# A hybrid encoder block on one core: the linear attention's decays move from the states to the queries, and the key norms' input moves to another ring

## The chip, the core and the metric

The kernel runs on one core of one Trainium2 chip. The metric is the device time of the whole program in microseconds (us). TensorE (PE) multiplies matrices into PSUM; VectorE (DVE), ScalarE (ACT) and GpSimd (POOL) work element by element; SyncE (SP) issues the DMAs here, all in one queue, in order. In the profile PEld is the loading of PE's weights.

## The reference

One layer of an encoder: 1024 tokens of width 1024, float32. Two branches work on the same normed projection, a linear attention with decays (4 heads, both directions) and a windowed attention (8 query heads, 2 key heads); their gated sum goes through a projection, and a SwiGLU network follows. What matters here is the linear attention and the norm of the windowed keys:

```python
    b = jnp.cumsum(log_g, axis=3)
    ...
    q_dec = q * jnp.exp(b)
    k_inv = k * jnp.exp(-b)
    k_tail = k * jnp.exp(b_last - b)
    ...
    def step(state, inp):
        kv_n, dec_n = inp
        return dec_n[..., None] * state + kv_n, state
    _, states = lax.scan(step, jnp.zeros(...), (chunk_kv, chunk_decay))
    o_inter = jnp.einsum("bhncd,nbhde->bhnce", q_dec, states)
    ...
    k = _rope(_rms_norm(k.astype(f32).reshape(bsz, s, hkv, hd), k_g), pos)
```

A query meets the state of the chunks before it (behind it, in the backward direction). The state is a 128x256 matrix for each head; each of its 128 rows has its own decay.

## The kernel before

Products run in pairs of `fp32r` parts: a weight unit (`wr`, 128x512) is split into `wh` by ScalarE and `wl` by VectorE, and three matmuls make one product. PE's instructions stand in the order in which the code is written; on the other engines a scheduler sets the order.

The stage of the change is the linear attention, about 338 to 557 us of the span. It goes by heads (`hd`, 4) and by chunks of 128 tokens (`c`, 8 a head), 32 in all, in numbered slots. In slot `n` stand `g_gates` for an even chunk and its neighbour (a pair shares `qk`, `e`, `cs`, `sm`, `q2`), one slot on `g_powers`, two on `g_scores`, four on `g_out`. When the last chunk of a head is through, `g_back_out` goes back over its chunks, and `g_turn` transposes the results `ob` two by two and writes them out by way of `ot`. Each slot is filled with matmuls of the projections that the next stages need (`fill`, 24 to 8 a slot, the list `dense`); these are the rows `mm<-wh,xh` and their like. So PE has work in every slot, but in a fixed order: where a matmul of the attention waits for its operand, all that is behind it waits too.

What the change touches:
- `sm` holds, for each pair, direction and chunk, the log decay from the edge of the chunk to its middle and from the middle to the other edge. Queries and keys are scaled with respect to the middle (`q2`, `en`).
- Forward, `g_out` makes `dec`, the decay from the middle of the chunk before to the middle of this one (one exponential of a column on ScalarE, L719), scales the state `pf` with it into `th` (ScalarE, L721), multiplies `th` by `q2[0]` (PE), and carries the state on: `pf = pf * dec + kv` (VectorE, L722).
- Backward, `g_back` does the same with `decb` (L741), `thb` (L743) and `kb` (L745), and `g_back_out` multiplies `thb` by `q2[1]`.
- `k_norm(t)` (eight of them, planned for slots 36 to 43) loads the keys of 128 tokens from `skv` into `kvr`, a ring of two buffers of its own (L784), norms and turns them on ScalarE and VectorE (L787 to L801), and writes `key` (L803). Since `kvr` is a ring of its own, the scheduler starts them as soon as `skv` is there; in the profile they run from 363 to 464 us.
- `qk` is the ring of two buffers into which `g_gates` loads a pair's queries and keys; `g_powers` reads it last.

Of the kernel before, what the change touches and what calls it, by code (L numbers as in the profile page):

```python
# [11 lines left out]
AF = mybir.ActivationFunctionType  # L12
ALU = mybir.AluOpType

P = 128
# [15 lines left out]
def body(tc, i, out):  # L31
    nc = tc.nc
    with ExitStack() as root:
# [8 lines left out]
        def nm(s):  # L42
            uid[0] += 1
            return f"{s}_{uid[0]}"
# [4 lines left out]
        def chtile(shape, dt=F32):  # L49
            return psc.tile(list(shape), dt, tag="ch", name=nm("ch"))  # L50
# [24 lines left out]
        def mm(o, a, b, start, stop):  # L75
            nc.tensor.matmul(o, a, b, start=start, stop=stop)  # L76

        def mm3(o, ah, al, bh, bl, start, stop):
            mm(o, ah, bh, start, False)
            mm(o, ah, bl, False, False)  # L80
            mm(o, al, bh, False, stop)
# [13 lines left out]
        def rsqrt(dst, v, scale, epsv, eps_t, pool, shape, tag, tags=None):  # L95
            tags = tags or (tag + "l", tag + "t")
            l = pool.tile(list(shape), F32, tag=tags[0], name=nm("rl"))
            nc.scalar.activation(l, v, AF.Ln, bias=eps_t[:, 0:1], scale=scale)
            nc.scalar.activation(l, l, AF.Exp, scale=-0.5)
            t = pool.tile(list(shape), F32, tag=tags[1], name=nm("rt"))  # L100
            nc.vector.tensor_scalar(t, v, scale, epsv, op0=ALU.mult, op1=ALU.add)
            nc.vector.tensor_tensor(t, t, l, op=ALU.mult)
            nc.vector.scalar_tensor_tensor(t, t, -0.5, l, op0=ALU.mult, op1=ALU.mult)
            nc.vector.scalar_tensor_tensor(dst, t, 1.5, l, op0=ALU.add, op1=ALU.mult)
# [10 lines left out]
        scr = {}  # L115
# [425 lines left out]
        with tc.manual_schedule(engines={mybir.EngineType.PE}):  # L541
# [8 lines left out]
            for k in range(KT):  # L550
# [5 lines left out]
                c = slice((k % 4) * P, (k % 4 + 1) * P)  # L556
# [63 lines left out]
        def gtile(tag, shape=(P, 256), dt=F32, bufs=2):  # L620
            return gt.tile(list(shape), dt, tag=tag, name=nm(tag), bufs=bufs)

        gla = {}
# [38 lines left out]
        def g_powers(hd, c):  # L662

            pr = gla[hd, c].pr
            qk, e, cs = pr.qk, pr.e, pr.cs
            ef, csf = (v.rearrange("p d j t -> p (d j t)") for v in (e, cs))
            nc.vector.tensor_tensor(e[:, 0], cs[:, 0], cs[:, 0, :, 63:64].to_broadcast([P, 2, P]), op=ALU.subtract)
            nc.vector.tensor_tensor(e[:, 1, :, 1:P], cs[:, 1, :, 0:P - 1], cs[:, 1, :, 63:64].to_broadcast([P, 2, P - 1]),
                                    op=ALU.subtract)
            nc.vector.tensor_scalar(e[:, 1, :, 0:1], cs[:, 1, :, 63:64], -1.0, None, op0=ALU.mult)  # L670

            x1 = cs.rearrange("p d j t -> p d (j t)")
            x2 = e.rearrange("p d j t -> p d (j t)")
            nc.scalar.activation(csf, ef, AF.Exp, scale=-1.0 / 16)
            nc.scalar.activation(ef, ef, AF.Exp, scale=1.0 / 16)
            pr.en = gtile("en", (P, 2, 256))
            nc.vector.tensor_tensor(pr.en[:, 0], x2[:, 0], qk[:, 1], op=ALU.mult)
            nc.vector.tensor_tensor(pr.en[:, 1], x1[:, 1], qk[:, 1], op=ALU.mult)
            pr.q2 = (gtile("q2f", bufs=3), gtile(f"q2b{c}", bufs=(3, 2, 2, 1)[c // 2]))
            nc.vector.tensor_tensor(pr.q2[0], x1[:, 0], qk[:, 0], op=ALU.mult)  # L680
            nc.vector.tensor_tensor(pr.q2[1], x2[:, 1], qk[:, 0], op=ALU.mult)
# [26 lines left out]
        def g_out(hd, c):  # L708

            a = gla[hd, c]  # L710
            kv = chtile((P, 2, 256))
            for d in range(2):
                mm3(kv[:, d], a.kth[:, d], a.ktl[:, d], a.vh, a.vl, True, True)
            a.pf = gtile("pf")
            if c:
                pf = gla[hd, c - 1].pf
                dec = gtile("dec", (P, 1))
                p = gla[hd, c - 1]
                nc.scalar.activation(dec, a.pr.sm[:, 0, a.j, 0:1], AF.Exp, bias=p.pr.sm[:, 0, p.j, 1:2])  # L719
                th = gtile("th")  # L720
                nc.scalar.activation(th, pf, AF.Copy, scale=dec[:, 0:1])  # L721
                nc.vector.scalar_tensor_tensor(a.pf, pf, dec[:, 0:1], kv[:, 0], op0=ALU.mult, op1=ALU.add)  # L722
                a.kb = gtile(f"kb{c}", bufs=2 if c < 5 else 1)
                nc.scalar.copy(a.kb, kv[:, 1])
            else:
                nc.vector.tensor_copy(a.pf, kv[:, 0])
                a.kb = None
            o = chtile((P, 256))
            mm3(o, a.sh, a.sl, a.vh, a.vl, True, c == 0)
            if c:  # L730
                mm(o, a.pr.q2[0][:, a.t], th, False, True)
            a.ob = gtile(f"ob{c}", bufs=2 if c < 5 else 1)
            nc.scalar.copy(a.ob, o)

        def g_back(hd, c):

            a = gla[hd, c]
            if c < NC - 1:
                n = gla[hd, c + 1]
                dec = gtile("decb", (P, 1))  # L740
                nc.scalar.activation(dec, a.pr.sm[:, 1, a.j, 1:2], AF.Exp, bias=n.pr.sm[:, 1, n.j, 0:1])  # L741
                a.thb = gtile("thb")
                nc.scalar.activation(a.thb, n.kb, AF.Copy, scale=dec[:, 0:1])  # L743
                if c:
                    nc.vector.scalar_tensor_tensor(a.kb, n.kb, dec[:, 0:1], a.kb, op0=ALU.mult, op1=ALU.add)  # L745

        def g_back_out(hd, c):
            a = gla[hd, c]
            if c < NC - 1:
                o2 = chtile((P, 256))  # L750
                mm(o2, a.pr.q2[1][:, a.t], a.thb, True, True)
                nc.vector.tensor_tensor(a.ob, a.ob, o2, op=ALU.add)
            if c:
                g_back(hd, c - 1)

            if c % 2:
                a.ss = gtile("oss", (P, 2))
            ss = a.ss if c % 2 else gla[hd, c + 1].ss
            sq = gtile("osq", bufs=1)
            nc.scalar.activation(sq, a.ob, AF.Square, accum_out=ss[:, 1 - c % 2:2 - c % 2])  # L760
            if c % 2 == 0:
                rs = gtile("ors", (P, 2))
                rsqrt(rs, ss, 1.0 / 256, EPS, epst, gt, (P, 2), "on")
                for j, v in enumerate((gla[hd, c + 1].ob, a.ob)):
                    nc.scalar.activation(v, v, AF.Copy, scale=rs[:, j:j + 1])
# [14 lines left out]
        def k_norm(t):  # L780

            need(("skv", t))
            raw = gtile("kvr", (P, 2, P))
            nc.sync.dma_start(out=raw.rearrange("p a b -> p (a b)"), in_=scr["skv", t][:, 0:256])  # L784
            b = gtile("sq2", (P, 2, P), bufs=1)
            ss = gtile("ss2", (P, 2))
            nc.scalar.activation(b, raw, AF.Square)  # L787
            nc.vector.tensor_reduce(ss, b, axis=mybir.AxisListType.X, op=ALU.add)
            rs = gtile("rs2", (P, 2))
            rsqrt(rs, ss, 1.0 / 128, EPS, epst, gt, (P, 2), "sn2")  # L790
            qn = gtile("qn2", (P, 2, P))
            for h in range(2):
                nc.vector.scalar_tensor_tensor(qn[:, h], raw[:, h], rs[:, h:h + 1], tb[0], op0=ALU.mult, op1=ALU.mult)
            c = tb[1][:, t:t + 1].to_broadcast([P, 2, 64])
            s = tb[2][:, t:t + 1].to_broadcast([P, 2, 64])
            nc.vector.tensor_tensor(b[:, :, 0:64], qn[:, :, 64:128], s, op=ALU.mult)
            nc.vector.tensor_tensor(b[:, :, 64:128], qn[:, :, 0:64], s, op=ALU.mult)
            nc.vector.tensor_tensor(qn[:, :, 0:64], qn[:, :, 0:64], c, op=ALU.mult)
            nc.vector.tensor_tensor(qn[:, :, 64:128], qn[:, :, 64:128], c, op=ALU.mult)
            nc.vector.tensor_tensor(qn[:, :, 0:64], qn[:, :, 0:64], b[:, :, 0:64], op=ALU.subtract)  # L800
            nc.vector.tensor_tensor(qn[:, :, 64:128], qn[:, :, 64:128], b[:, :, 64:128], op=ALU.add)  # L801
            scr["key", t] = scratch(f"key_{t}", (P, 256))
            nc.sync.dma_start(out=scr["key", t], in_=qn.rearrange("p a b -> p (a b)"))  # L803
# [3 lines left out]
        for n in range(NH * NC):  # L807
            hd, c = divmod(n, NC)
# [11 lines left out]
        with tc.manual_schedule(engines={mybir.EngineType.PE}):  # L820
            fill(24)
            for t in range(last + 1):
                n = 24 if t < 2 else 16 if t < 4 else 12 if t < NH * NC + 4 else 8 if t < last - 1 else 18
# [189 lines left out]
        for n in range(2 * KT):  # L1013
            g, t = divmod(n, KT)
# [522 lines left out]
```

## Time and profile before

| what | value |
|---|---|
| time, median of 3 runs | 1645.47 us (1645.38 to 1646.94) |
| the profiled execution's own time | 1645.61 us |
| its span, first to last instruction | 1643.8 us |
| granted TensorE clock | 1.000 |
| `th` (L721) and `thb` (L743), ScalarE, 28 each | 515 and 510 ns (medians) |
| `pf` (L722), 28, and `kb` (L745), 24, VectorE | 476 and 482 ns (medians) |
| bytes moved | 262.91 MB, mean 160 GB/s |

How to read it: a row of the timeline has start and duration in us, engine, line, operation, written tile `<-` read tiles, and in brackets how long the engine sat idle before it and who ended that. In a group's row stand the count, busy us and mean ns. A line such as L76 or L72 is that of a helper (`mm`, `wunit`), so that the tiles' names tell what is meant.

### The profile page before, as it was taken

How to read it: one execution, taken by the hardware profiler on the slowest of the kernel's cores; microseconds unless marked ns; L12 is line 12 of the kernel's file. 1: busy time of each engine (PE TensorE's matmuls, PEld its weight loads, DVE VectorE, ACT ScalarE, POOL GpSimd, SP SyncE). 2: the span in 40 equal slices, each digit the busy share in tenths (PEclk: the TensorE clock that was granted, in tenths of full speed). 3: DMA queues.
4: the chain of work that ended last, by engine and by line, in shares of the span. 5: the costliest groups of instructions: out<-in, count | busy, mean ns of one | idle time of the engine just before them, and what ended most of it. 6: DMA issues, size and time to landing. Idle time of an engine off the chain costs nothing.

```text
span 1643.8 us, 23281 instructions
## 1 busy us (share of the span) xinstructions
PE 1626.0 (99%) x7588; PEld 1346.0 (82%) x7588; DVE 1251.4 (76%) x2559; ACT 842.6 (51%) x1762; POOL 76.0 (5%) x68
## 2 busy tenths in 40 slices
PE   9999999999999989999999999999999999999999
PEld 7888888888888778888888888888888888888887
DVE  8866665589986598867885678887777778779655
ACT  8622224468998666665554557333333333354442
POOL 0000000000000034540000000000000000000000
PEclk9999999999999999999999999999999999999999
DMA  7554334475554633248765544443334443596433
GB/s 238 176 178 148 115 122 135 173 250 173 179 161 129 191 108 97 77 138 280 225 205 175 168 146 145 140 149 109 109 115 147 142 147 129 177 341 193 149 98 119
DMA packets 168010, 262.91 MB, mean 160 GB/s; under 512 B 19324, under 2 KB 52860, under 8 KB 167888
## 3 DMA queue, kind: packets, MB, share of 16 engines
q1 hardware_dynamic: 167888, 261.42, 49.8%
q8 instruction: 60, 0.98, 0.2%
q14 instruction: 62, 0.51, 0.1%
HBM read 187.93 MB, written 73.42 MB: 159 GB/s over the span
## 4 chain that ended last, share of the span: by engine, by line
PE 84%; DVE 9%; ACT 4%; DMA 2%; issue 1%; POOL 1%; SPq 0%; ACTq 0%; DVEq 0%
PE mm L76 23%; PE mm L306 9%; PE mm L308 9%; PE mm L307 9%; PE mm L1350 7%; PE ch L1350 5%; PE ch L76 4%; PE ch L306 4%; PE ch L308 4%; PE ch L307 4%; PE ch L460 3%; PE mm L460 2%; ACT p L956 1%; DVE wl L72 1%; DVE cs L655 1%
## 5 line engine op out<-in xcount | busy, mean ns | idle before, releaser
L298 ACT ACTIVATE wh<-ws 128x512 fp32r<-128x512 f32 x132 | 83.3, 632 | 195.9 <-PE mm L307 102.2
L70 ACT ACTIVATE wh<-wr 128x512 fp32r<-128x512 f32 x202 | 124.9, 626 | 87.4 <-PE mm L76 54.9
L72 DVE TENSOR_TENSOR wl<-wr,wh 128x512 fp32r<-128x512 f32 x202 | 137.7, 686 | 26.8 <-ACT wh L70 26.4
L299 DVE TENSOR_TENSOR wl<-ws,wh 128x512 fp32r<-128x512 f32 x132 | 90.5, 686 | 22.7 <-ACT wh L298 22.6
L298 ACT ACTIVATE wh<-wr 128x512 fp32r<-128x512 f32 x69 | 43.6, 632 | 124.8 <-issue 49.7
L962 POOL TENSOR_SCALAR p<-p,rd 128x384 f32<-128x384 f32 (+1 forms) x64 | 75.8, 1202 | 657.1 <-DMA qr<-sq 587.2
L298 ACT ACTIVATE wh<-a 128x512 fp32r<-128x512 f32 x64 | 40.5, 633 | 91.4 <-PE ch L1350 42.3
L76 PE MATMUL mm<-wh,xl 128*128 128x512 f32 x192 | 83.1, 433 | 0.0
L76 PE MATMUL mm<-wh,xh 128*128 128x512 f32 x192 | 79.6, 415 | 0.0
L76 PE MATMUL mm<-wl,xh 128*128 128x512 f32 x192 | 79.6, 414 | 0.0
L299 DVE TENSOR_TENSOR wl<-a,wh 128x512 fp32r<-128x512 f32 x64 | 44.2, 691 | 43.1 <-ACT wh L298 42.5
L1350 PE MATMUL mm<-hh,wh 128*128 128x512 f32 x176 | 68.5, 389 | 0.0
L1350 PE MATMUL mm<-hl,wh 128*128 128x512 f32 x176 | 68.5, 389 | 0.0
L1350 PE MATMUL mm<-hh,wl 128*128 128x512 f32 x176 | 68.5, 389 | 0.0
L76 PE MATMUL mm<-xl,wh 128*128 128x512 f32 x160 | 64.5, 403 | 0.1
L76 PE MATMUL mm<-xh,wh 128*128 128x512 f32 x160 | 64.4, 403 | 0.2 <-ACT wh L70 0.2
L76 PE MATMUL mm<-xh,wl 128*128 128x512 f32 x160 | 59.2, 409 | 0.0
L1320 DVE TENSOR_TENSOR hl<-hr,hh 128x512 fp32r<-128x512 f32 x75 | 51.4, 685 | 3.7 <-ACT hh L1319 3.7
L1350 PE MATMUL ch<-hh,wh 128*128 128x512 f32 x132 | 51.3, 389 | 0.0
L1350 PE MATMUL ch<-hl,wh 128*128 128x512 f32 x132 | 51.3, 389 | 0.0
L1350 PE MATMUL ch<-hh,wl 128*128 128x512 f32 x132 | 51.3, 389 | 0.0
L76 PE MATMUL mm<-oah,wh 128*128 128x512 f32 x128 | 50.2, 392 | 0.0
(620 smaller groups left out, 5077.7 us busy)
## 6 DMA issues: line engine op xcount, KB each, us to landing
wr<-in_w_fi_dram SPq DMA_DIRECT2D x102, 256.0 KB
wr<-in_w_f_dram SPq DMA_DIRECT2D x80, 256.0 KB
wr<-in_w_t_dram SPq DMA_DIRECT2D x56, 256.0 KB
B<-c SPq DMA_DIRECT2D x44, 256.0 KB
T<-tx SPq DMA_DIRECT2D x44, 256.0 KB
a<-in_w_fo_dram SPq DMA_DIRECT2D x44, 256.0 KB
hr<-T SPq DMA_DIRECT2D x44, 256.0 KB
wr<-in_w_ob_dram SPq DMA_DIRECT2D x32, 256.0 KB
```

Source lines behind the costliest of these rows:

```text
L70: nc.scalar.activation(h, raw, AF.Copy)
L72: nc.vector.tensor_tensor(l, raw, h.bitcast(F32), op=ALU.subtract)
L76: nc.tensor.matmul(o, a, b, start=start, stop=stop)
L298: nc.scalar.activation(h, src, AF.Copy)
L299: nc.vector.tensor_tensor(l, src, h.bitcast(F32), op=ALU.subtract)
L306: nc.tensor.matmul(o, h[:, c], x[kk][0], start=start and kk == 0, stop=False, skip_group_check=True)
L307: nc.tensor.matmul(o, h[:, c], x[kk][1], start=False, stop=False, skip_group_check=True)
L308: nc.tensor.matmul(o, l[:, c], x[kk][0], start=False, stop=kk == nk - 1, skip_group_check=True)
L460: nc.tensor.matmul(ys[m], a[:, c], b, start=f0, stop=f1, skip_group_check=True)
L962: nc.gpsimd.tensor_scalar(p[:, h, :w], p[:, h, :w], rd[:, h:h + 1], None, op0=ALU.mult)
L1320: nc.vector.tensor_tensor(l, r, h.bitcast(F32), op=ALU.subtract)
L1350: nc.tensor.matmul(ys[m], a[:, c], b, start=f0, stop=f1, skip_group_check=True)
```

## The change

The decays of a pair, forward and backward, are now made in `g_powers`, in one tile `dec`: two small sums on VectorE (one in the first pair of a head) and one exponential on ScalarE. `g_out` and `g_back` no longer scale the state. They multiply the 128x128 block of queries in place by the same column (VectorE), behind the scores that read it unscaled, and PE multiplies it by the unscaled state `pf` or `kb`. `k_norm` loads all 512 columns of `skv` into a buffer of the ring `qk` and uses the first 256; `kvr`, `th`, `thb` and `decb` are gone.

```diff
@@ g_powers
+            pr.dec = gtile("dec", (P, 2, 2), bufs=16)
+            nc.vector.tensor_tensor(pr.dec[:, 1], pr.sm[:, :, 1, 0], pr.sm[:, :, 0, 1], op=ALU.add)
+            if c:
+                nc.vector.tensor_tensor(pr.dec[:, 0], pr.sm[:, :, 0, 0], gla[hd, c - 1].pr.sm[:, :, 1, 1], op=ALU.add)
+            dc = pr.dec[:, 0 if c else 1:2]
+            nc.scalar.activation(dc, dc, AF.Exp)
@@ g_out
-                dec = gtile("dec", (P, 1))
-                p = gla[hd, c - 1]
-                nc.scalar.activation(dec, a.pr.sm[:, 0, a.j, 0:1], AF.Exp, bias=p.pr.sm[:, 0, p.j, 1:2])
-                th = gtile("th")
-                nc.scalar.activation(th, pf, AF.Copy, scale=dec[:, 0:1])
-                nc.vector.scalar_tensor_tensor(a.pf, pf, dec[:, 0:1], kv[:, 0], op0=ALU.mult, op1=ALU.add)
+                dec = a.pr.dec[:, a.j, 0:1]
+                q = a.pr.q2[0][:, a.t]
+                nc.vector.tensor_scalar(q, q, dec, None, op0=ALU.mult)
+                nc.vector.scalar_tensor_tensor(a.pf, pf, dec, kv[:, 0], op0=ALU.mult, op1=ALU.add)
...
-                mm(o, a.pr.q2[0][:, a.t], th, False, True)
+                mm(o, q, pf, False, True)
@@ g_back
-                dec = gtile("decb", (P, 1))
-                nc.scalar.activation(dec, a.pr.sm[:, 1, a.j, 1:2], AF.Exp, bias=n.pr.sm[:, 1, n.j, 0:1])
-                a.thb = gtile("thb")
-                nc.scalar.activation(a.thb, n.kb, AF.Copy, scale=dec[:, 0:1])
+                dec = (n if a.j else a).pr.dec[:, 1 - a.j, 1:2]
+                q = a.pr.q2[1][:, a.t]
+                nc.vector.tensor_scalar(q, q, dec, None, op0=ALU.mult)
+                a.after = n.kb
                 if c:
-                    nc.vector.scalar_tensor_tensor(a.kb, n.kb, dec[:, 0:1], a.kb, op0=ALU.mult, op1=ALU.add)
+                    nc.vector.scalar_tensor_tensor(a.kb, n.kb, dec, a.kb, op0=ALU.mult, op1=ALU.add)
@@ g_back_out
-                mm(o2, a.pr.q2[1][:, a.t], a.thb, True, True)
+                mm(o2, a.pr.q2[1][:, a.t], a.after, True, True)
@@ k_norm
-            raw = gtile("kvr", (P, 2, P))
-            nc.sync.dma_start(out=raw.rearrange("p a b -> p (a b)"), in_=scr["skv", t][:, 0:256])
+            qk = gtile("qk", (P, 2, 256))
+            raw = qk[:, 0].rearrange("p (a b) -> p a b", a=2)
+            nc.sync.dma_start(out=qk.rearrange("p a b -> p (a b)"), in_=scr["skv", t])
```

PE's order stays, but for the names of two operands a chunk and a handful of neighbouring rows; on ACT there are 1534 rows where there were 1630. What follows shows the scheduler's order, without times.

First ScalarE in the middle of the stage (second head's forward pass, first head's return; in the trace of before 402.7 to 406.5 us). Before:

```order
L733 COPY ob_930_4156<-ch_4151 128x256
L99 ACTIVATE rl_4117<-rl_4117 128x2
L741 ACTIVATE decb_4401<-sm_3274 128x1
L724 COPY kb_928_4149<-ch_4136 128x256
L695 ACTIVATE kth_4168<-ch_4165 128x256
L721 ACTIVATE th_4233<-pf_4143,dec_4231 128x256
L701 COPY sp_4175<-ch_4172 128x128
L719 ACTIVATE dec_4341<-sm_3867 128x1
L765 ACTIVATE ob_868_3969<-ob_868_3969,ors_4116 128x256
L765 ACTIVATE ob_847_3894<-ob_847_3894,ors_4116 128x256
L648 ACTIVATE e_4191<-ch_4188 128x512
L743 ACTIVATE thb_4315<-kb_795_3728,decb_4313 128x256
```

Now, at the same place:

```order
L738 COPY ob_917_4152<-ch_4147 128x256
L98 ACTIVATE rl_4116<-oss_4035,eps 128x2
L729 COPY kb_915_4145<-ch_4135 128x256
L99 ACTIVATE rl_4116<-rl_4116 128x2
L702 ACTIVATE kth_4164<-ch_4161 128x256
L708 COPY sp_4171<-ch_4168 128x128
L770 ACTIVATE ob_860_3970<-ob_860_3970,ors_4115 128x256
L770 ACTIVATE ob_840_3894<-ob_840_3894,ors_4115 128x256
L648 ACTIVATE e_4187<-ch_4184 128x512
```

The two scalings and the two exponentials of a chunk are gone from between the copies that empty PSUM (`ob`, `kb`, `kth`, `sp`).

Second VectorE a little earlier in the first head, where the rows of a key norm (`ss`, `rt`, `qn`, `sq`) stood between those of a chunk (`ktl`, `sp`, `sh`, `sl` from the scores; `pf` the state). Before:

```order
L722 SCALAR_TENSOR_TENSOR pf_3795<-pf_3722,dec_3796,ch_3788 128x256
L72 TENSOR_TENSOR wl_3983<-wr_3979,wh_3981 128x512
L800 TENSOR_TENSOR qn_1629_6366<-qn_1629_6366,sq_1624_6353 128x2x64
L801 TENSOR_TENSOR qn_1629_6366<-qn_1629_6366,sq_1624_6353 128x2x64
L696 TENSOR_TENSOR ktl_3834<-ch_3830,kth_3833 128x256
L788 TENSOR_REDUCE ss_1640_6403<-sq_1639_6402 128x2
L702 COPY_PREDICATED sp_3840<-tri,ch_3837 128x128
L101 TENSOR_SCALAR rt_6410<-ss_1640_6403 128x2
L705 CAST sh_3843<-sp_3840 128x128
L706 TENSOR_TENSOR sl_3844<-sp_3840,sh_3843 128x128
```

Now:

```order
L727 SCALAR_TENSOR_TENSOR pf_3801<-pf_3728,dec_3482,ch_3794 128x256
L72 TENSOR_TENSOR wl_3984<-wr_3980,wh_3982 128x512
L726 TENSOR_SCALAR q2f_3640<-q2f_3640,dec_3631 128x128
L703 TENSOR_TENSOR ktl_3837<-ch_3833,kth_3836 128x256
L709 COPY_PREDICATED sp_3843<-tri,ch_3840 128x128
L712 CAST sh_3846<-sp_3843 128x128
L713 TENSOR_TENSOR sl_3847<-sp_3843,sh_3846 128x128
```

The norm's rows are gone from here, and one multiplication of queries stands in their place.

Third VectorE in the last head's return: from the sum `ob` of the second pair to the norm `ors` of that pair, on which its transposition waits. Before (539.08 to 541.63 us):

```order
L752 TENSOR_TENSOR ob_1513_5989<-ob_1513_5989,ch_6448 128x256
L72 TENSOR_TENSOR wl_6669<-wr_6665,wh_6667 128x512
L101 TENSOR_SCALAR rt_6462<-oss_6387 128x2
L752 TENSOR_TENSOR ob_1492_5927<-ob_1492_5927,ch_6505 128x256
L102 TENSOR_TENSOR rt_6462<-rt_6462,rl_6459 128x2
L103 SCALAR_TENSOR_TENSOR rt_6462<-rt_6462,rl_6459 128x2
L104 SCALAR_TENSOR_TENSOR ors_6458<-rt_6462,rl_6459 128x2
```

Now:

```order
L757 TENSOR_TENSOR ob_1441_5917<-ob_1441_5917,ch_6352 128x256
L72 TENSOR_TENSOR wl_6561<-wr_6557,wh_6559 128x512
L794 TENSOR_REDUCE ss_1610_6534<-sq_1609_6533 128x2
L101 TENSOR_SCALAR rt_6363<-oss_6291 128x2
L757 TENSOR_TENSOR ob_1424_5861<-ob_1424_5861,ch_6406 128x256
L102 TENSOR_TENSOR rt_6363<-rt_6363,rl_6360 128x2
L101 TENSOR_SCALAR rt_6541<-ss_1610_6534 128x2
L103 SCALAR_TENSOR_TENSOR rt_6363<-rt_6363,rl_6360 128x2
L102 TENSOR_TENSOR rt_6541<-rt_6541,rl_6538 128x2
L104 SCALAR_TENSOR_TENSOR ors_6359<-rt_6363,rl_6360 128x2
```

The reduction and small rows of a key norm (`ss`, `rt_6541`) now stand among those of the pair. The tensor rows of a norm stand ahead of the first `ob` and behind `ors`. On SP the norms' loads (`qk<-skv`) now stand between the last loads of values, the writes of `ot` and the loads of weights, the last of the eight ahead of the writes of the first pair of this return.

## The prediction

> **What bounds the kernel now.** I read the page first: the span and the busy table.
>
> ```profile
> span 1643.8 us, 23281 instructions
> PE 1626.0 (99%) x7588; PEld 1346.0 (82%) x7588; DVE 1251.4 (76%) x2559; ACT 842.6 (51%) x1762; POOL 76.0 (5%) x68
> ```
>
> TensorE (PE) is busy for 99% of the span. The change leaves every matmul in place, so it can only win time in which PE waits, and only where its code runs. The next view is busy time by stretch; each row gives a stretch, its length, then busy us and instructions of PE, weight loads, DVE, ACT and POOL.
>
> ```profile
> 363.00:465.00 102.00, 100.56 (x588) 85.36 (x587) 98.71 (x356) 90.43 (x271) 0.00 (x0) 1.00 0.57 172
> 465.00:505.00 40.00, 39.54 (x233) 33.81 (x232) 34.21 (x108) 36.78 (x111) 0.00 (x0) 1.00 0.50 150
> 505.00:557.00 52.00, 51.46 (x269) 42.62 (x268) 25.77 (x78) 43.34 (x130) 0.00 (x0) 1.00 0.45 141
> 557.00:565.00 8.00, 8.00 (x37) 6.61 (x36) 1.39 (x2) 1.02 (x3) 0.00 (x0) 1.00 0.83 262
> ```
>
> The first three hold the linear attention but for its start; the fourth leads to the windowed attention. The first has the key norms: VectorE is busy 98.71 of 102 us, ScalarE 90.43. In the second both still have about nine tenths. In the third, the return of the last head, VectorE has half its time free.
>
> PE's own idle time here is small (1.44, 0.46 and 0.54 us), but a stalled PE still counts the running matmul as busy. The waits of the weight loads (390 to 560 us) say who ends its stalls; the columns are total, times and longest:
>
> ```profile
> PEld ch L76 <- ACT ob L733: 3.5, 6, 0.9
> PEld ch L771 <- ACT ob L765: 1.3, 2, 0.9
> PEld ch L771 <- DVE ktl L696: 1.3, 2, 0.7
> PEld ch L76 <- DVE ktl L696: 1.3, 4, 0.5
> PEld ch L76 <- ACT kb L724: 1.1, 3, 0.5
> ```
>
> That is 8.5 us in 17 waits. To see what one costs, the largest in the timeline, first PE, then the weight loads:
>
> ```profile
> 401.95 0.39 PE L76 MATMUL mm<-wh,xh 128*128 128x512 f32 x1
> 402.18 0.40 PE L76 MATMUL mm<-wl,xh 128*128 128x512 f32 x1
> 403.08 0.50 PE L76 MATMUL ch<-lrS,upS 98*128 98x256 f32 x2 [0.50 <-ACT ob L733]
> ...
> 403.08 0.30 PEld L76 LDWEIGHTS ch<-lrS,upS 98*128 98x128 f32 x2 [0.93 <-ACT ob L733]
> ```
>
> Matmuls start 0.23 us apart (401.95 to 402.18); this gap is 0.90, so 0.67 us is lost where 0.93 is listed, and 0.26 of a listed wait is ordinary. Over all: 8.5 - 17 x 0.26 = **4.1 us lost in this stage**. The waits that ACT ends (5.9 us, 11 times) make 3.0 of it, those that DVE ends (2.6, 6 times) 1.0. This is all that can be won here: 0.25% of the time.
>
> **What the change removes.** On ScalarE, per chunk, two scalings of a 128x256 state (`th`, `thb`) and two one-column exponentials. Rows of the whole run, minimum/median/maximum in ns:
>
> ```profile
> L721 ACT ACTIVATE th<-pf,dec x28: 498/515/572, 355.1 to 523.4; 128x256 f32<-128x256 f32 x28
> L719 ACT ACTIVATE dec<-sm x16: 281/298/343, 338.0 to 520.5; 128x1 f32<-128x1 f32 x16
> ...
> L743 ACT ACTIVATE thb<-kb,decb x28: 493/510/535, 393.3 to 544.3; 128x256 f32<-128x256 f32 x28
> ```
>
> A scaling with its exponential is 0.51 + 0.30 = 0.8 us, and 56 x 0.8 = 45 us leave ScalarE; 16 exponentials of two or four columns come back (16 x 0.3 = 5 us).
>
> **What it adds.** 56 in-place multiplications of a 128x128 query block by a column on VectorE, and 28 two-column sums. The trace has no such multiplication. Its bounds are a tiny row and one of four times the elements; the nearest by size and by a single input is the cast. Rows of DVE in 363 to 465 us, with count, busy us and mean ns:
>
> ```profile
> L72 DVE TENSOR_TENSOR wl<-wr,wh 128x512 fp32r<-128x512 f32 x18 | 12.3, 685 | 0.0
> L696 DVE TENSOR_TENSOR ktl<-ch,kth 128x256 fp32r<-128x256 f32 x18 | 7.5, 418 | 0.4 <-ACT kth L695 0.3
> L650 DVE TENSOR_SCALAR e<-e 128x512 f32<-128x512 f32 x10 | 4.2, 422 | 0.4 <-ACT e L648 0.4
> L705 DVE CAST sh<-sp 128x128 fp32r<-128x128 f32 x18 | 4.0, 223 | 0.1
> L788 DVE TENSOR_REDUCE ss<-sq 128x2 f32<-128x256 f32 x7 | 2.9, 409 | 0.0
> L103 DVE SCALAR_TENSOR_TENSOR rt<-rt,rl 128x2 f32<-128x2 f32 x14 | 2.2, 157 | 0.1
> ```
>
> I take 0.22 us (0.16 to 0.42): 56 x 0.22 = 12 us (9 to 24), and 28 x 0.16 = 4.5 us for the sums. One tensor input of 512 columns takes 422 ns (L650), two take 685 (L72). [...]
>
> **What it moves.** The eight key norms, now all in 363 to 465 us, get their input in the ring of `qk` (two buffers) and can only start once the last pairs' powers have been read from it, in the third stretch. Their tensor rows stand back to back in one place:
>
> ```profile
> 461.70 0.34 DVE L793 SCALAR_TENSOR_TENSOR qn<-kvr,rs,kg 128x128 f32<-128x128 f32 x1
> ...
> 463.63 0.42 DVE L696 TENSOR_TENSOR ktl<-ch,kth 128x256 fp32r<-128x256 f32 x1
> ```
>
> Eight rows in 1.93 us; with the reduction (0.41) and four small rows, less their overlap, about 2.6 us each, 21 us for eight. On ScalarE a norm has a Square and two tiny rows, some 0.9 us.
>
> **The new balance**, from the table of stretches:
> - 363 to 465: 18 chunks (one `ktl` each, row above) of 5.7 us, with some 30 multiplications, as the first chunk of a head has none forward and its way back starts late. DVE 98.7 - 21 + 30 x 0.22 + 18 sums x 0.16 = 87 of 102. ACT 90.4 - 30 x 0.8 - 7 (norms) + 3 = 62. Both come free.
> - 465 to 505 (7 chunks): DVE 34.2 + 14 x 0.22 + 1.1 = 38.4 of 40 (41.2 at the upper bound, 1.2 us too much); ACT 36.8 - 14 x 0.8 + 1 = 27.
> - 505 to 557: DVE 25.8 + 21 + 12 x 0.22 = 49.4 of 52; ACT 43.3 - 10 + 7 = 40.
>
> So ACT's stalls before 505 go. Of the 3.0 us, one lies behind that point:
>
> ```profile
> 536.13 0.40 PE L76 MATMUL mm<-wl,xh 128*128 128x512 f32 x1
> 537.02 0.44 PE L771 MATMUL ch<-ident,ob 128*128 128x128 f32 x2 [0.49 <-ACT ob L765]
> ```
>
> That gap of 0.89 loses 0.66 and stays; **2.3 us** go. `ktl` comes sooner with DVE relieved, but is behind ACT's `kth` too: I take half of its 1.0, **0.5 us**.
>
> **The end of the stage is where it may be paid back.** The way from a sum `ob` over its norm to the transposition of the pair has no room:
>
> ```profile
> 536.26 0.16 DVE L104 SCALAR_TENSOR_TENSOR ors<-rt,rl 128x2 f32<-128x2 f32 x1
> ...
> 539.08 0.42 DVE L752 TENSOR_TENSOR ob<-ob,ch 128x256 f32<-128x256 f32 x1 [2.26 <-PE ch L76]
> ...
> 541.47 0.16 DVE L104 SCALAR_TENSOR_TENSOR ors<-rt,rl 128x2 f32<-128x2 f32 x1
> ...
> 541.85 0.39 PE L76 MATMUL mm<-wh,xl 128*128 128x512 f32 x1
> 542.23 0.44 PE L771 MATMUL ch<-ident,ob 128*128 128x128 f32 x2
> ```
>
> The transposition starts 0.38 us behind the matmul ahead of it, 0.15 more than usual: it is already late. In the new order a reduction (0.41) and three small rows of a norm come between this sum and `ors` (539.08 to 541.47), beside the weight part that was there; DVE stood idle for about as much in those 2.4 us. In the third pair two rows of 0.34 and three small ones stand between; I count **0.4 us** for it.
>
> SyncE's queue (SP) runs in order, and a norm's load of `qk` waits for the norm two before it; output writes and weight loads stand behind. The last such load waits for the sixth norm's first two tensor rows, which now stand right behind the first pair's `ors`: 536.26 + 0.16 + 2 x 0.34, about 537.1. The writes behind it follow a transposition that comes after 537.02 and a copy of it, so the load holds up nothing. Each brings 512 columns where 256 were needed: eight times 128 KB more, 1 MB in all, in a stretch where 52 us x 141 GB/s = 7.3 MB move. Behind the stage comes a pause of VectorE (1.39 us busy in 557 to 565) before the windowed attention's first work:
>
> ```profile
> 565.05 0.69 DVE L859 TENSOR_TENSOR qA<-cosb,qg 128x512 f32<-128x512 f32 x1 [2.53 <-DMA sink<-in_sink_dram]
> ```
>
> Its constants (`cosb` to `sink`) queue behind the last write of `ot`, so they follow PE's last transposition, not the norms, and the keys are written ahead of that write. So what is behind moves forward together. Norms that were late past 557 would be covered for 6.6 us (8 - 1.39).
>
> Sum: -2.3 - 0.5 + 0.4 = **-2.4 us**. The profiled execution took 1645.61 us (span 1643.8 and 1.8 around it), 0.14 above the median 1645.47; from the median, **1643.1 us**.
>
> **Rivals.**
> - *All stalls go.* With both engines under their limit in every stretch, PE never waits: -4.1, 1641.4 us. For it: ACT falls to 62 of 102. Against: 49.4 of 52 at the end, in an order that cannot yield. [...] No stretch here runs at 95% without waits.
> - *VectorE takes ACT's place.* Waits for ACT copies become waits for a DVE that stays 95% full from 465 on: the 2.8 gained give back 1.2 (the upper bound of the multiplication) and 4 x 0.4 at the turns: 1645.5 us.
> - *Slower:* in the last head's return each pair of slots needs its norm's ACT results in DVE's queue, and DVE waits there. If its 1.93 us block is late at each of the four turns, 7.7 us are added: 1645.5 - 2.8 + 7.7 = 1650.4 us. It turns the sign from 0.7 us a turn. For it: no room at the turn. Against: the rows place the block behind `ors`.
> - That the change does not do what it says is ruled out by the order: 96 rows fewer on ACT, the norms behind the last pair.
>
> **Chances.** Forecast 0.45 (its own range 1641.8 to 1644.5), all stalls 0.27, VectorE 0.19, slower 0.09. A measurement here tells 0.2% (3.3 us) from no change, so faster means under 1642.2: 0.27 and 0.06 of the forecast's share, 0.33; slower 0.09; the rest, 0.58, within. The range, 1640.2 to 1646.8, leaves out the slower case and the edges: it reaches 1.2 under the case of all stalls, as the 4.1 rests on one gap, and to 1.3 above the case of VectorE, for the multiplication's upper bound.
>
> **What would show it.** The waits on `ob` L733 gone from the weight loads' list before 505; DVE near 87 of 102 and ACT near 62 in the first stretch; the multiplication near 0.22 us; the norms between 505 and 552; and at most 0.5 us more at the turns. Wrong would be new waits of PE for `q2f` or `ob` ended by DVE, or a first `qA` that comes late against PE.

## The result, and the profile after

The changed kernel takes **1649.43 us** (median of 9 runs, 1648.22 to 1651.68) against 1645.43 for the kernel before in the same runs (9 runs, 1644.91 to 1646.94): ratio 1.0024, 95% interval 1.0016 to 1.0033. It is 4.0 us slower, where 2.4 us less was forecast, and the time lies outside the range. The profiled execution took 1648.76 us, of which the span is 1647.0.

The head of the page, span and busy table:

```profile
span 1647.0 us, 23287 instructions
...
PE 1627.4 (99%) x7588; PEld 1346.7 (82%) x7588; DVE 1263.7 (77%) x2643; ACT 817.3 (50%) x1666; POOL 76.0 (5%) x68
```

VectorE (DVE) is busy for 12.3 us more, with 84 instructions more, ScalarE (ACT) for 25.3 us less. The table of stretches, with the same columns as before:

```profile
363.00:465.00 102.00, 101.00 (x590) 85.93 (x589) 90.12 (x306) 73.43 (x201) 0.00 (x0) 1.00 0.51 155
465.00:505.00 40.00, 39.15 (x229) 32.53 (x227) 35.60 (x122) 31.12 (x90) 0.00 (x0) 1.00 0.49 152
505.00:557.00 52.00, 50.30 (x263) 41.56 (x262) 45.15 (x191) 40.29 (x126) 0.00 (x0) 1.00 0.61 188
```

VectorE fell from 98.71 to 90.12 in the first stretch and rose from 25.77 to 45.15 in the third, as the move of the norms should make it; ScalarE fell in all three, from 90.43, 36.78 and 43.34. PE is nevertheless busy for less of the second and third stretch than before (39.15 and 50.30 us against 39.54 and 51.46). The waits from 390 to 560 us, the largest of the weight loads and one of ScalarE:

```profile
ACT kb L729 <- DVE pf L727: 5.9, 9, 1.1
...
PEld ch L76 <- ACT kb L729: 3.7, 7, 0.8
...
PEld ch L776 <- ACT ob L770: 2.4, 2, 1.2
...
PEld ch L776 <- DVE ktl L703: 1.5, 2, 0.8
...
PEld ch L76 <- DVE ktl L703: 1.1, 2, 0.6
```

The waits on the copy of `ob` (L738 now; 3.5 us in 6 times before) are gone. In their place PE waits for ScalarE's copy of `kb`: 3.7 us in 7 waits, where it was 1.1 in 3. And that copy itself waits for VectorE's `pf`, 5.9 us in 9 waits. Before, ScalarE had this wait too:

```profile
ACT kb L724 <- DVE pf L722: 4.1, 9, 1.0
```

But it lay elsewhere. Between 420 and 505 us it was 1.2 us in 4 waits and is now 5.7 in 8; PE's waits for the copy there were 0.7 us in 2 and are now 2.9 in 5. One such place, first in the profile after (start, length, engine, line, operation):

```profile
483.98 0.60 PE L76 MATMUL ch<-pf,q2f 128*128 128x256 f32 x2
...
485.58 0.48 DVE L727 SCALAR_TENSOR_TENSOR pf<-pf,dec,ch 128x256 f32<-128x256 f32 x1
...
486.09 0.37 ACT L729 COPY kb<-ch 128x256 f32<-128x256 f32 x1 [0.26 <-DVE pf L727]
...
486.36 0.38 ACT L738 COPY ob<-ch 128x256 f32<-128x256 f32 x1
...
486.51 0.50 PE L76 MATMUL ch<-lrS,upS 98*128 98x256 f32 x2 [0.34 <-ACT kb L729]
```

The last matmul into the buffer of `o` runs at 483.98. ScalarE then does nothing for 0.26 us ahead of `kb`, which starts 0.03 us behind the end of `pf` (485.58 + 0.48 = 486.06); the copy of `ob` stands behind `kb` in ScalarE's order, and PE's next projection into a `ch` buffer (`lrS`) starts at 486.51, when `kb` has ended. The same place before:

```profile
483.00 0.60 PE L76 MATMUL ch<-th,q2f 128*128 128x256 f32 x2
...
484.95 0.47 DVE L722 SCALAR_TENSOR_TENSOR pf<-pf,dec,ch 128x256 f32<-128x256 f32 x1
485.02 0.35 ACT L733 COPY ob<-ch 128x256 f32<-128x256 f32 x1
...
485.43 0.51 PE L76 MATMUL ch<-lrS,upS 98*128 98x256 f32 x2 [0.23 <-ACT ob L733]
...
485.82 0.35 ACT L724 COPY kb<-ch 128x256 f32<-128x256 f32 x1
```

There `ob` was copied ahead of `kb`, at 485.02, while VectorE still worked on `pf`; `lrS` started right behind it, at 485.43. The same matmul is now 1.08 us later, but 0.97 of that had gathered ahead of this place; here PE's gap is 0.74 us, where it was 0.63. Which copy goes first is the scheduler's order: it is `kb` for 17 of the 28 chunks now, for 15 before.

Both kernels run the same 7588 matmuls in the same order, so the start of each can be compared with its start before, in PE's timeline; the growth of this lag over a stretch is what the stretch lost (the stretches are those of before). Every profile of this study, in us, the last column being the timed median less that of the kernel before, run beside it:

| kernel | to 340 | 340-420 | 420-505 | 505-557 | 557-605 | 605-end | sum | timed |
|---|---|---|---|---|---|---|---|---|
| after | 0.58 | -1.31 | 1.99 | 1.21 | 0.84 | -0.14 | 3.2 | +4.0 |
| after_again | 1.12 | -1.32 | 1.96 | 1.18 | 1.49 | 1.71 | 6.1 | +5.2 |
| after_third | -0.21 | -1.29 | 1.95 | 1.18 | 1.67 | 0.28 | 3.6 | +3.4 (one run) |
| norms_alone | 0.65 | -1.33 | 0.32 | 1.10 | -0.51 | -0.46 | -0.2 | -0.2 |
| decays_alone | 0.46 | -0.36 | 0.91 | -0.20 | 0.14 | 0.44 | 1.4 | +1.0 |
| mult_on_scalar | -0.27 | -1.32 | 1.59 | 1.83 | -0.34 | -0.49 | 1.0 | +2.1 |
| kb_first | -0.39 | -1.69 | 0.13 | 0.87 | 0.81 | -0.60 | -0.9 | -0.1 |
| kb_first_again | 0.17 | -1.80 | 0.14 | 0.86 | -0.15 | -0.45 | -1.2 | -1.4 (one run) |
| before_kb_first | 0.52 | 0.13 | 0.93 | -0.28 | 0.62 | -0.26 | 1.7 | +0.7 |
| no_norm | 0.62 | -1.81 | 0.10 | -0.86 | -0.51 | -0.24 | -2.7 | -1.6 |
| norms_later | 0.03 | -1.81 | 0.10 | 0.94 | -0.65 | -0.39 | -1.8 | -0.6 |
| norms_paired | 0.28 | -1.81 | 0.10 | 1.79 | -0.05 | -0.38 | -0.1 | +1.1 |
| early_norms_kb_first | 1.23 | -0.80 | 0.21 | -0.65 | 1.03 | -0.48 | 0.5 | -1.3 |

A row's sum belongs to its profiled execution, which can lie well off its kernel's median (`early_norms_kb_first` 1646.17 us, median 1643.68; `before_kb_first` 1647.25, 1645.51; `after_again` 1651.74, 1650.03). From 340 to 557 us a kernel repeats itself within 0.11 us in each stretch (three profiles of the changed kernel, two of `kb_first`). The start, where the code is the same in all, and the stretches behind 557 vary more. So the change lost 1.9 us in the linear attention (-1.3 + 2.0 + 1.2), and 0.8 to 1.7 in the 48 us behind it.

### The profile page after: what moved, and what is told of

It is laid out like the page before. It is cut to its first block, busy times and chain, and to the rows that moved or that the text cites. A ratio compares the mean times of both kernels' runs of the same rounds, so it can differ in the third digit from the quotient of the medians.

```text
span 1647.0 us, 23287 instructions
## 1 busy us (share of the span) xinstructions
PE 1627.4 (99%) x7588; PEld 1346.7 (82%) x7588; DVE 1263.7 (77%) x2643; ACT 817.3 (50%) x1666; POOL 76.0 (5%) x68
## 4 chain that ended last, share of the span: by engine, by line
PE 84%; DVE 8%; ACT 4%; DMA 1%; issue 1%; POOL 1%; SPq 0%; DVEq 0%; ACTq 0%
PE mm L76 23%; PE mm L306 9%; PE mm L308 9%; PE mm L307 9%; PE mm L1356 7%; PE ch L1356 5%; PE ch L76 4%; PE ch L308 4%; PE ch L306 4%; PE ch L307 4%; PE ch L460 3%; PE mm L460 2%; ACT p L962 1%; DVE wl L72 1%; DVE cs L655 1%
```

## The experiments

**The two halves of the change.** `decays_alone` is the changed kernel with the norms' old input:

```diff
-            qk = gtile("qk", (P, 2, 256))
-            raw = qk[:, 0].rearrange("p (a b) -> p a b", a=2)
-            nc.sync.dma_start(out=qk.rearrange("p a b -> p (a b)"), in_=scr["skv", t])
+            raw = gtile("kvr", (P, 2, P))
+            nc.sync.dma_start(out=raw.rearrange("p a b -> p (a b)"), in_=scr["skv", t][:, 0:256])
```

> Decays as in the changed kernel, key norms with the ring of `kvr` as before (so they run beside the earlier heads again). Theory 1 (VectorE's multiplications and the copies of `kb` that start behind `pf` hold PE's buffers): VectorE would need 98.7 + 33 x 0.28 + 16 x 0.15 = 110 of the 102 us of 363 to 465, so 6 to 9 us slower than before, 1651 to 1654. Theory 2 (the loss lies in the norms behind the last pair, the decays gain as predicted): 2 us faster than before, about 1643. Theory 3 (neither part; the loss lies in the first 10 us and at the start of the windowed attention by chance): as before, 1645.

Measured: 1645.99 us, ratio 1.0006 (0.9998 to 1.0015). The 6 to 9 us of theory 1 did not come. Its row for the first stretch:

```profile
363.00:465.00 102.00, 100.52 (x585) 85.22 (x584) 100.00 (x376) 74.76 (x217) 0.00 (x0) 1.00 0.55 167
```

VectorE is full, but 376 rows stand there where 356 of before and 49 new ones (33 multiplications, 16 sums) were to fit: others slid behind 465, where 142 and 102 rows stand against 108 and 78 before, with some 35 new ones to be expected. PE lost little by it. Nor did theory 2 come true: the decays by themselves win 0.36 us up to 420 and lose 0.91 behind it.

`norms_alone` is the kernel before with the opposite edit, the norms through the ring of `qk`.

> Decays as before, key norms through the ring of `qk` as in the changed kernel. Theory 1: VectorE is relieved by 21 us in 363 to 465 and needs 47 of 52 in 505 to 557; the late turns cost 0.4 to 1.3 us, the waits on `ktl` go: 1645 to 1647. Theory 2: the norms cost what the changed kernel lost and what the decays should have won, 4 + 2.4 us: about 1652. Theory 3: as before, 1645.

Measured: 1644.81 us, ratio 0.9999 (0.9991 to 1.0008). By its profile it wins 1.33 us between 340 and 420, as much as the whole change does there, keeps 1.0 of that up to 505 and pays 1.10 in 505 to 557. Its waits from 390 to 560:

```profile
PEld ch L771 <- ACT ob L765: 3.0, 3, 1.9
...
PEld ch L76 <- ACT ob L733: 1.7, 2, 0.9
```

The waits on the copy of `ob` fell from 3.5 us to 1.7 with ScalarE's scalings still in place: for the one at 403.08 that the prediction shows, the norms' leaving was enough. ScalarE's relief takes this wait away too, but wins nothing by it: in `decays_alone` PE loses 0.83 us seven matmuls earlier instead, at 402.84, where VectorE's sum `ob` ends the wait. The waits of the transpositions on `ob` rose from 1.3 to 3.0.

By time each half alone is no different from the kernel before, as theory 3 had it; only together are they slower. But the loss is not chance at the start: from 420 to 505 the halves lose 0.91 and 0.32 us, the two together 1.99, and two more profiles of the changed kernel repeat it. ScalarE's wait for `pf` ahead of `kb` between 420 and 505 tells them apart: 4.8 us in 7 waits in `decays_alone`, 1.2 in 4 in `norms_alone`, as before. So it grows where ScalarE is rid of the scalings. Why the two halves cost more than their sum is open.

**Who holds the copy of `kb`?** In `kb_first` two statements of the changed kernel change places:

```diff
-                nc.vector.scalar_tensor_tensor(a.pf, pf, dec, kv[:, 0], op0=ALU.mult, op1=ALU.add)
                 a.kb = gtile(f"kb{c}", bufs=2 if c < 5 else 1)
                 nc.scalar.copy(a.kb, kv[:, 1])
+                nc.vector.scalar_tensor_tensor(a.pf, pf, dec, kv[:, 0], op0=ALU.mult, op1=ALU.add)
```

> The changed kernel with the copy of `kb` written ahead of the update of `pf`; both read one PSUM tile. If the two reads of one tile are put one behind the other, the copy no longer waits for VectorE but `pf` waits for the copy. Theory 1 (the wait of `kb` behind `pf` holds the PSUM ring): PE's losses ahead of `lrS` (1.4 us between 420 and 490) go: about 1648. Rival (the end of the two reads stays where it is, since `pf` is now behind): within 0.5 us of 1649.4.

Measured: **1644.89 us**, ratio 0.9999 (0.9990 to 1.0008), 4 to 5 us below the changed kernel (-0.1 against +4.0 and +5.2 in the last column), and 3 us below what theory 1 expected. The lag between 420 and 505 fell from 1.99 us to 0.13. The place shown above, in this kernel:

```profile
481.36 0.60 PE L76 MATMUL ch<-pf,q2f 128*128 128x256 f32 x2
...
482.30 0.38 ACT L728 COPY kb<-ch 128x256 f32<-128x256 f32 x1
...
482.65 0.38 ACT L738 COPY ob<-ch 128x256 f32<-128x256 f32 x1
...
482.94 0.47 DVE L729 SCALAR_TENSOR_TENSOR pf<-pf,dec,ch 128x256 f32<-128x256 f32 x1
...
483.38 0.40 PE L76 MATMUL ch<-lrS,upS 98*128 98x256 f32 x2
```

Now `kb` is copied first and `ob` right behind it, 0.69 us after the matmuls into its buffer have ended (481.36 + 0.60 to 482.65; it was 1.78 us in the changed kernel, 1.42 before), and `pf` comes last. `lrS` starts at 483.38, before `pf` has ended: it takes the buffer that `ob` set free. So the wait did not just change sides. ScalarE has work queued behind the copy that PE waits for; that VectorE has less of it behind `pf` is argued, not measured. What is left of it in the weight loads' waits (390 to 560) is smaller, 1.7 us on `pf` where 3.7 were on `kb`:

```profile
PEld ch L776 <- ACT ob L770: 2.8, 3, 1.3
...
PEld ch L76 <- DVE pf L729: 1.7, 3, 0.7
```

This is not all of the loss, however. The growth of the lag from 420 to 505, by the matmuls at which it arises:

| kernel | `lrS` | `kb,q2b` (`thb,q2b` before) | transpositions of `ob` | others | sum |
|---|---|---|---|---|---|
| after | 0.67 | 1.38 | 0.30 | -0.36 | 1.99 |
| kb_first | -0.39 | 1.08 | -0.81 | 0.26 | 0.13 |

PE's waits ahead of `lrS` end with the copy of `kb`. Ahead of `kb,q2b`, a product of the return, the two longest waits end with VectorE's `ktl`, which needs ScalarE's `kth`; and ScalarE now has an exponential of the gates (`cs`) in front of `kth`. After, then before:

```profile
480.44 0.63 ACT L681 ACTIVATE cs<-e 128x512 f32<-128x512 f32 x1 [0.30 <-DVE e L670]
...
480.98 0.37 ACT L702 ACTIVATE kth<-ch 128x256 fp32r<-128x256 f32 x1
...
481.91 0.30 PEld L76 LDWEIGHTS ch<-kb,q2b 128*128 128x128 f32 x2 [0.57 <-DVE ktl L703]
```

```profile
478.69 0.43 ACT L695 ACTIVATE kth<-ch 128x256 fp32r<-128x256 f32 x1
...
480.10 0.63 ACT L674 ACTIVATE cs<-e 128x512 f32<-128x512 f32 x1 [0.97 <-DVE e L670]
```

Of the eight such exponentials between 420 and 505, none stood ahead of its neighbour `kth` before; six do in the changed kernel and four in `kb_first`, and what `kb,q2b` loses lies at these alone. So `kb_first` does not take away all that the changed kernel lost: it keeps most of this part, and at the other matmuls it is faster than the kernel before. No run turns `cs` and `kth` alone.

> `kb_first` once more, for a second profile beside it. In 340 to 505 a gain of 1.6 us against before and in 505 to 557 a loss of 0.9, as in its first; the landing 3.6 us by theory B, anything from 3.0 to 4.9 by theory A; the granted clock of 565 to 605 (0.96 in the first) is 0.96 again if it belongs to the kernel, 1.00 if it varies.

Measured: 1644.36 us (one run, the kernel before 1645.76 beside it). The stretches from 340 to 557 repeat those of the first profile; the landing took 3.64 us, and the clock was 1.00.

The same two statements turned in the kernel before (`before_kb_first`; there `th` and its exponential stay ahead of both):

> The kernel before, with nothing changed but that the copy of `kb` is written ahead of the update of `pf`. Theory A (the copy that stands behind `pf` on ScalarE is a cost of the changed kernel alone, since before, `ob` was often copied first): between 0.5 us faster and no change, 1644.5 to 1645. Theory B (the same wait cost the kernel before as much, and the gain of `kb_first` over the changed kernel is a gain by itself): 2 us faster, about 1643. Theory C (`pf` is now late for its reader): slower by 1 us or more.

Measured: 1645.51 us, ratio 1.0005 (0.9996 to 1.0014). No gain; in the profile 1.06 us are lost from 340 to 505. So the order of the two reads is no improvement by itself: it is the changed kernel that needs it.

**Do the multiplications on VectorE cost it?** `mult_on_scalar`, both places:

```diff
-                nc.vector.tensor_scalar(q, q, dec, None, op0=ALU.mult)
+                nc.scalar.activation(q, q, AF.Copy, scale=dec)
```

> The changed kernel with the 56 query multiplications on ScalarE (a scaled copy in place, 128x128) instead of VectorE. Theory 1: VectorE loses 16 us of work, ScalarE gets some 15 us; PE's losses ahead of `lrS` and `kb` between 420 and 510 fall by 1 to 2 us: 1647 to 1648.5. Theory 2: no change, 1649.4. A third possibility (ScalarE becomes the bound again): 1650 or more.

Measured: 1647.06 us, ratio 1.0014 (1.0005 to 1.0023), as theory 1 forecast, but not for its reason: 340 to 505 loses only 0.4 us less than in the changed kernel, and 505 to 557 loses 0.6 more. The rest of the difference is in the stretches that vary. The multiplications are a small part of the loss. (`cs` stands ahead of `kth` six times here too, and `kb,q2b` loses 1.54 us.)

**What costs 1.2 us at the return?** `no_norm` is `kb_first` without the norms' arithmetic:

```diff
-            b = gtile("sq2", (P, 2, P), bufs=1)
...
-            nc.vector.tensor_tensor(qn[:, :, 64:128], qn[:, :, 64:128], b[:, :, 64:128], op=ALU.add)
+            qn = raw
```

> As `kb_first`, but the key norms are left out: each tile of keys is loaded into the ring of `qk` and written out as it is, without the Square, the reduction, the scalings and the rotation. Theory A (the norms' rows between a sum and its `ors` make the turns late): the 1.3 us lost in 505 to 557 go, 1643.5. Rival (the transfers, or something else in that stretch): no change, 1644.9.

Measured: 1643.19 us, ratio 0.9989 (0.9980 to 0.9997). Against `kb_first` the third stretch gains 1.73 us (0.87 to -0.86), more than expected, though the transfers are all still there. Of its waits on the scaled sums one is left, that of the first turn:

```profile
PEld ch L776 <- ACT ob L770: 0.7, 1, 0.7
```

So the norms' rows, not their bytes, make the turns late. Two attempts at a better place for them, both on `kb_first`:

```diff
-            at[NH * NC + 4 + t, 7] = (k_norm, t)
+            at[NH * NC + 6 + t, 7] = (k_norm, t)
```

> As `kb_first`, with every key norm two slots later, so that the last end in VectorE's pause ahead of the windowed attention. Theory A (two norms fewer lie ahead of the first late turn): a loss of 1.0 us at the first turn falls by half, the pause covers the rest: 1644.3. Rival (the later turns are hit instead, or the last keys come too late for the windowed attention): no change or up to 2 us slower, 1645 to 1647.

Measured: 1644.21 us, ratio 0.9997 (0.9988 to 1.0006); the third stretch still loses 0.94 us. The first turn is not relieved: the gap of PE ahead of it loses 1.19 us, 1.06 in `kb_first`.

```diff
-            at[NH * NC + 4 + t, 7] = (k_norm, t)
+            at[NH * NC + 4 + t // 2 * 2, 7 + t % 2] = (k_norm, t)
...
-                slot([(lambda v=at[t, j]: v[0](*v[1:])) if (t, j) in at else None for j in (0, 6, 5, 4, 3, 2, 1, 7)], n)
+                slot([(lambda v=at[t, j]: v[0](*v[1:])) if (t, j) in at else None for j in (0, 6, 5, 4, 3, 2, 1, 7, 8)], n)
```

> As `kb_first`, with two key norms in every other slot, that of the odd chunk, instead of one in each, so that none is emitted in the slot of a pair's second sum. Theory A (what costs 1.3 us in 505 to 557 is rows of a norm between a pair's second sum and its `ors`): the loss falls to 0.7 us or less, 1644.3. Rival (VectorE simply has too much to do at the turns, in whatever order): 1.3 us or more stay, 1645 to 1646.

Measured: 1646.14 us, ratio 1.0005 (0.9996 to 1.0014), and 1.79 us lost in the third stretch, 0.9 more than in `kb_first`: theory A's remedy made it worse. The slot in which a norm is written does not keep its rows off the chain; that two norms in a row stand there as one larger block is likely, but was not followed up.

**Both repairs.** `early_norms_kb_first` is `decays_alone` with the two reads turned as in `kb_first`.

> Decays as in the changed kernel, the copy of `kb` written ahead of the update of `pf`, key norms early with the ring of `kvr` (as `decays_alone`, with the order of the two reads turned). Theory A (the wait of the copy behind `pf` and the norms at the return are the two losses, each by itself): against `decays_alone` 1.5 to 2 us less in 340 to 505, nothing lost in 505 to 557; 1643.5 to 1644.5. Rival (with the norms there VectorE is full, 100 of 102 us, and the turned order only moves PE's waits from the copy to `pf`): as `decays_alone`, 1646.

Measured: 1643.68 us, ratio 0.9993 (0.9984 to 1.0002), 2.3 us below `decays_alone`. It gains 1.1 us against it up to 505 (0.55 to -0.59, less than expected) and loses nothing in the third stretch. It is the fastest version with the whole computation, but no faster than the kernel before by what these runs can tell.

**The changed kernel again.**

> The changed kernel once more, unchanged, for a second profile. Theory A: PE loses 0.6 us against before in 340 to 505 us and 1.3 in 505 to 557 again, since these come from the order of the instructions; what it lost in the first 10 us (0.6) and ahead of the windowed attention's first transpositions (0.8) may come out otherwise; median within 1 us of 1649. Rival: the 0.8 us ahead of the windowed attention stays too, and belongs to the change.

Measured: 1650.03 us (7 runs), ratio 1.0029 (1.0018 to 1.0040). From 340 to 557 us it repeats itself; 557 to 605 lost 1.49.

> The changed kernel, for a third profile: from the issue of the `sink` load to the first `qA`, 4.46 and 4.92 us in its first two profiles against 3.0 to 4.2 in the other kernels', though the same loads are issued in the same order ahead of it. Theory A (the landing there varies from execution to execution): it can come out near 3.6, and the 0.8 to 1.5 us lost in 557 to 605 with it. Theory B (it belongs to the changed kernel): 4.4 or more again, and 0.8 us or more lost. In both: about 0.65 us lost in 340 to 505 and 1.2 in 505 to 557.

Measured: 1649.17 us (one run). The landing took 4.16 us, between the two theories' figures, and 1.67 us were lost in 557 to 605, at a granted clock of 0.96 in 565 to 605 where the first two profiles have 1.00 (below).

## Why the prediction was wrong, point by point

**"ACT's stalls before 505 go", -2.3, and half of `ktl`'s, -0.5: this is the step that failed.** Measured from 340 to 505: +0.65 (three profiles). Its first part came: -1.3 up to 420, where two of the larger waits on `ob` lay; but `norms_alone` wins just that with the scalings in place, and `decays_alone` only 0.36, so the norms' leaving was enough and ScalarE's relief was not. Behind 420 came 2.0 us of loss, and PE's waits on `ktl` stayed at 2.6 us in all. The step argued from the busy share: ScalarE at 62 of 102 us would hold nobody up. But ScalarE does its rows in the scheduler's order, and in front stands the copy of `kb`, which waits until VectorE has read the other half of the same PSUM buffer for `pf`: at the place shown above the last matmul for `ob` had ended at 484.58 us, and `ob` was copied behind `kb`, at 486.36. The waits of before had the row for it (4.1 us in 9 waits), and the prediction counted PE's waits on that copy (1.1 us) among those that ScalarE ends. Once the states' scalings no longer filled ScalarE, it stood there longer, 5.7 us for 1.2 between 420 and 505, and of the 28 copies 26 start within 0.1 us of the end of `pf`, before 19. `kb_first` takes this one wait away, and the loss falls by 1.8 of the 2.0 us. That is a net figure: 1.1 us that come behind `kth` stay and are outweighed. That the order of `cs` and `kth` costs them is read from the rows and not tested.

The two halves of `kv` are one tile of 2 x 256 fp32 columns, and in all 14 profiles the two reads stay at least 0.03 us apart, whichever is written first (0.03 us at the place shown above in the changed kernel, 486.06 to 486.09, and 0.26 in `kb_first`, where `kb` ends at 482.68 and `pf` starts at 482.94). What two reads at the same time would do no run here shows.

**The new balance.** Forecast for VectorE 87, 38.4 and 49.4 us in the three stretches, measured 90.12, 35.60 and 45.15; for ScalarE 62, 27 and 40, measured 73.43, 31.12 and 40.29. ScalarE's 11 us in the first stretch are an error of method. Its 271 rows there add up to 114.9 us before, in 90.43 us of busy time: neighbouring rows overlap. After, 201 rows add up to 86.9 in 73.43. The rows fell by 28 us, as forecast, the busy time by only 17. Durations cannot be subtracted from a busy time. The terms for VectorE's own new rows, from 363 to 465:

```profile
L747 DVE TENSOR_SCALAR q2b<-q2b,dec 128x128 f32<-128x128 f32 x17 | 4.6, 279 | 0.0
...
L726 DVE TENSOR_SCALAR q2f<-q2f,dec 128x128 f32<-128x128 f32 x16 | 4.5, 281 | 0.4 <-PE ch L76 0.4
...
L673 DVE TENSOR_TENSOR dec<-sm 128x2 f32<-128x2 f32 x9 | 1.4, 152 | 0.0
```

The sums cost 0.15 us (0.16 forecast), the multiplication 0.28 where 0.22 was taken, inside its bounds. By the 0.06 the 56 of them cost 3.4 us of VectorE's time, which `mult_on_scalar` shows to be of little weight.

**"At most 0.4 us at the turns": right mechanism, wrong size.** 1.2 us. The first turn, which was to stay at 0.66, lost 0.94, and the third 0.91 where nothing was lost before. The third turn after:

```profile
545.12 0.59 PE L76 MATMUL ch<-kb,q2b 128*128 128x256 f32 x2
545.26 0.68 DVE L72 TENSOR_TENSOR wl<-wr,wh 128x512 fp32r<-128x512 f32 x1
...
545.86 0.41 DVE L794 TENSOR_REDUCE ss<-sq 128x2 f32<-128x256 f32 x1
...
546.19 0.41 DVE L757 TENSOR_TENSOR ob<-ob,ch 128x256 f32<-128x256 f32 x1
...
546.30 0.30 ACT L98 ACTIVATE rl<-ss,eps 128x2 f32<-128x2 f32 x1 [0.51 <-DVE ss L794]
...
546.74 0.40 ACT L765 ACTIVATE osq<-ob 128x256 f32<-128x256 f32 x1
...
547.46 0.35 DVE L799 SCALAR_TENSOR_TENSOR qn<-qk,rs,kg 128x128 f32<-128x128 f32 x1
...
547.73 0.41 DVE L757 TENSOR_TENSOR ob<-ob,ch 128x256 f32<-128x256 f32 x1
...
548.72 0.15 DVE L104 SCALAR_TENSOR_TENSOR ors<-rt,rl 128x2 f32<-128x2 f32 x1
...
549.65 0.44 PE L776 MATMUL ch<-ident,ob 128*128 128x128 f32 x2 [0.75 <-ACT ob L770]
```

and before:

```profile
543.64 0.59 PE L76 MATMUL ch<-thb,q2b 128*128 128x256 f32 x2
...
544.27 0.42 DVE L752 TENSOR_TENSOR ob<-ob,ch 128x256 f32<-128x256 f32 x1 [0.46 <-PE ch L76]
...
544.79 0.42 ACT L760 ACTIVATE osq<-ob 128x256 f32<-128x256 f32 x1
...
546.35 0.16 DVE L104 SCALAR_TENSOR_TENSOR ors<-rt,rl 128x2 f32<-128x2 f32 x1
...
547.28 0.38 PE L771 MATMUL ch<-ident,ob 128*128 128x128 f32 x2
```

From PE's matmul for the second sum to the transposition it was 3.64 us (543.64 to 547.28) and is 4.53: 0.89 more. Half of it (0.44) lies ahead of the sum `ob`, which stood behind the reduction `ss` of a norm and a weight part; the other half between the Square `osq` and `ors` (1.56 us before, 1.98 after), where a `qn` of the norm and the next pair's sum come in between. ScalarE waits for the norm's `ss` too, ahead of `osq`. The prediction had counted rows between the sum and `ors` only, and only those of VectorE. (For the second pair it took VectorE's idle time for as long as the new rows; it is 0.45 us for 0.89 of rows, and yet that turn lost nothing.) Against the rival without a loss here it had set VectorE's 49.4 of 52 us; at 45.15 the loss came all the same: this chain, without slack, was late though the engine was not full. `no_norm` shows it to be the norms.

**"What is behind moves forward together": not quite.** The constants of the windowed attention are issued as far behind PE as before, 2.45 us later like PE's matmuls there, but the last of them lands later. After, then before (the row of `qA` before is in the prediction):

```profile
563.91 0.43 SPq L63 DMA_DIRECT2D sink<-in_sink_dram  x1
...
568.37 0.69 DVE L865 TENSOR_TENSOR qA<-cosb,qg 128x512 f32<-128x512 f32 x1 [3.38 <-DMA sink<-in_sink_dram]
```

```profile
561.46 0.43 SPq L63 DMA_DIRECT2D sink<-in_sink_dram  x1
```

From the load of `sink` to the first `qA` it takes 4.46 us (4.92 and 4.16 in the other two profiles), against 3.59 before, 4.15 in `decays_alone` and 3.04 to 3.79 in all other kernels, though the same loads go ahead of it in the same order. What slows the landing is **open**. It was not the norms' bytes: `kb_first` moves the same ones, with 3.60 and 3.64.

**The rivals.** "VectorE takes ACT's place" was right in kind: waits for copies became waits that end with VectorE. But VectorE is 89 and 87% full behind 465, not 95%, and the rival gave back only what had been gained, by the length of the multiplication and the turns; the actual way, through the order of ScalarE's rows, gave back 2.0 us before the turns. "All stalls go" is ruled out. The slower rival had another mechanism, the norms' block late at every turn: it is late at two, by 0.3 and 0.9 us instead of 1.93, and not enough alone to turn the sign (`kb_first` has the same norms).

**What stays open.** Besides the two orders on ScalarE, which no run separates: the located losses are 2.7, 3.3 and 3.5 us (340 to 605, three profiles), the timed ones 4.0 and 5.2. Part of the rest may be other late transfers: in two of the changed kernel's three profiles PE stalls by 0.4 and 1.4 us near 975 us, far behind the change, in no other kernel's; in `after_again` 1.7 us were lost behind 605, where ten profiles of other kernels lie between -0.60 and +0.44. No run here tells why.

## What to carry to other kernels

A wait has to be followed through its releaser to the engine that ends it: if the copy that PE waits for is itself waiting, relief for the copying engine can just let it stand there longer (here 5.7 us for 1.2 between 420 and 505). Where two engines read one PSUM buffer here, their order in the program decided which queue stood still: from 390 to 560 us ScalarE waited 5.9 us for `pf` in the changed kernel, and VectorE 0.8 us for `kb` in `kb_first`. Which should go first has to be tried: the same turn was worth 1.8 us of the lag in the changed kernel and nothing in the kernel before. Work that was moved into a stretch with room (VectorE ended at 45.15 of 52 us) was paid on the chains that cross it, 1.2 us; such chains have to be priced row by row on every engine that the work uses.

## What the runs showed that was not expected

The multiplication of 128x128 elements by a column takes 0.28 us, like a multiplication of two tensors of this size (0.287 in the rows of before), and more than the cast (0.22). The 512-column row with a constant (`e<-e`, 0.42 us) does four times the elements in 1.5 times the time. Work in place is not the reason by itself, since that row works in place too; whether the column is the reason was not tried.

The granted clock fell to 0.96 within the windowed attention's first part in 5 of the 14 profiles, each of another kernel. Two profiles of `kb_first`, the same stretch (the third number from the right is the clock):

```profile
565.00:605.00 40.00, 35.65 (x178) 28.64 (x176) 37.39 (x124) 26.26 (x71) 9.04 (x8) 0.96 0.47 138
```

```profile
565.00:605.00 40.00, 35.12 (x183) 28.18 (x182) 38.37 (x125) 26.71 (x73) 9.30 (x9) 1.00 0.47 142
```

At 0.96 the lag grew by 0.81 us in 557 to 605, at 1.00 by -0.15; but `norms_later` has -0.65 at 0.96. So a single profile's loss there is uncertain by about 1 us, and how much of it is the clock's is open.
